# A 64x64 triangular inverse by back substitution on VectorE, corner block included, in a FoX / RWKV-7 layer

## The chip, the cores and the metric

The kernel runs on one core of one Trainium2 chip. A core has a matrix engine (TensorE, PE in the profile, with its weight loads as PEld), VectorE (DVE), ScalarE (ACT), GpSimd (POOL), and SyncE (SP), whose queue issues nearly all transfers. The metric is the device time of one execution in microseconds (us). Before the change the median of three runs is 1895.11 us (1894.64 to 1896.51).

## The reference

One layer over 256 tokens of width 4096. A joint input projection feeds 16 attention heads with a forget gate (FoX, head width 128), 32 RWKV-7 heads (head width 64) and a gate; the gated outputs go through an output projection, a residual and a LayerNorm.

```
proj = x @ w_in                       # 4096 -> fox q|k|v|f, rwkv r|k|v|w_down|a_down, gate z
fox  = softmax(q k^T / sqrt(128) + c_t - c_s, causal) v        # c = cumsum(log_sigmoid(f + f_bias))
S_t  = S_{t-1} diag(w_t) + (S_{t-1} a_t) b_t^T + v_t k_t^T      # 64x64 state of each rwkv head
y_t  = S_t r_t                        # then GroupNorm per head, plus a bonus term
out  = concat(fox, rwkv) * silu(z) @ w_out
x    = LayerNorm(ALPHA * x + out)
```

The recurrence of the RWKV heads is computed in chunks of 64 tokens. In a chunk the terms S a of the 64 tokens depend on each other through a strictly triangular 64x64 matrix N; the kernel forms (1 - N)^-1 for each head and chunk, called X, and then needs only matrix products.

## The kernel before

**Staging.** The 4096-deep projections are products of 128x128 by 128x512 on PE. Every operand is split in two parts, a rounded one (h) made by ScalarE and the rest (l) made by VectorE, and each product is done as three (h h, l h, h l). The weights stream in as tiles of 128x1024 (two steps of the depth): loaded by SP into `raw` buffers (tag `wr`, 6 of them, in `load` and `fetch`), split by `split` into `wh` (4 buffers) and `wl` (3). A tile feeds twelve products.

The input projection runs as 8 groups of 4 blocks (`block(n, b)`), 512 columns each. Group n carries the columns of two FoX heads and of four RWKV heads, as two pairs u = 0, 1 of heads j = 0, 1. `unload` turns a block's result and stores it to memory and back, to have the tokens along the free axis. Then the output projection goes over 8 column blocks of 16 tiles (`project`).

**Side work.** Between the products of the projections stands the work on the heads: `prepare(i)` forms decays and scaled keys of one pair (with `front`), `rwkv(n)` does the chunked recurrence of the four heads of a group ("pass n", 8 passes), `fox(i)` one attention head, `gate` multiplies by the gate, splits and stores a 128-column piece `hl` (29 of the 32 pieces go to memory and come back as `h`; the last three stay).

**The pass.** `rwkv(n)` forms gp, the products of keys with keys and queries of a chunk, masks them into gb and lt, and sends the diagonal 32x32 blocks of N through memory (`nd`) to a layout (`nb`, tag `Nb`) in which 16 matrices lie over the 128 partitions, 8 partitions each, four columns per partition. There the back substitution runs: 31 steps of a multiply (`prod <- Nb, xc`) and a reduction (`xc <- prod`) on VectorE, for two head pairs at once, on 8 columns of each: four of the inverse of a diagonal block, and four of the product of that inverse with the corner block of N, which comes through `zd`. The two results go back through memory (`td`, `qd`) into the tile `TQ`. VectorE transposes the T part into the diagonal blocks of X; TensorE multiplies Q by the other diagonal block (`xp`: 16 products of 32x32 per pass, two instructions each), and ScalarE and VectorE copy that into the corner of X. Then the chunks follow in order: a residual R (`rh`), u = X R (`up`), the state (`sp`), and for all four chunks together the output `yp`. In the first chunk the residual is done in four halved products per pass, beside the xp products; in the later chunks by two full ones per pass.

`residual`, for c > 0 and for c = 0:

```
for u in range(2):
    nc.tensor.matmul(rh[:, u * P : (u + 1) * P], both[:, u, c, 0].rearrange("p j t -> p (j t)"), states[:, :, u, c, :], start=True, stop=True)
...
for u in range(2):
    for j in (1, 0):
        nc.tensor.matmul(rh[HALF[j], u * C : (u + 1) * C], lt[j][:, u, c, 0], SV[j][:, u, c, :], start=True, stop=True)
```

**What sets the order.** Nothing is issued while the program above runs. The class `Later` records every operation of every engine with a duration that it works out from its shape, and `flush` then plans a start for each: at every moment the engine that is free first takes the ready operation with the smallest key. The key is the place of recording, with the splits of weights put far ahead. The generators (`prepare`, `rwkv`, `fox`, `unload`) yield at each `slot()`, two of which stand in each tile, so how often one yields sets its keys. `ROWS` is how many steps of the substitution are recorded in one slot. Side products on PE that follow each other are planned as one run; a change of tile shape on PE costs in the plan. All operations are issued in the planned order by one line of `flush`, line 372, which is why every row of the profile names L372.

Buffers are tiles with a tag; two tiles of a tag share its buffers. `lt`, `BK`, `eL`, `sums` and `above` have one buffer each, `t` five.

**The end.** The output projection needs all pieces h, and the last ones come from pass 7. So `outs` lists first the tiles 0 to 13 (`CUT`) of column blocks 0 and 1, then the first `EARLY` tiles of block 2, and only then tiles 14 and 15 of blocks 0 and 1. When block 0 is complete, the memory of the side work is closed and that of the LayerNorm opened; `load_tok(b)` loads what the residual and LayerNorm of block b need.

Of the kernel before, what the change touches and what calls it, by code (L numbers as in the profile page):

```python
# [19 lines left out]
P = 128  # L20
# [22 lines left out]
EARLY = 4  # L43
BACK = 10
ROWS = 1
# [423 lines left out]
def layer(ctx: ExitStack, tc: tile.TileContext, xt, xtok, w_first, w_main, muv, w_o, up, par, mulora, fbias, lng, lnb, cst, out):  # L469
# [109 lines left out]
    sums = const.tile([P, B], F32, name="sums")  # L579
    nc.gpsimd.memset(sums, 0.0)  # L580
    above = const.tile([P, B // 2], F32, name="above")
    nc.gpsimd.memset(above, 0.0)
# [86 lines left out]
    def rt(name):  # L669
        return t256("t", name, 5)  # L670
# [32 lines left out]
    def lora():  # L703
# [5 lines left out]
        u = rp.tile([NF, S], F32, tag="t", name="fu", bufs=5)  # L709
# [15 lines left out]
    def forget():  # L725
        def ft(name):
            return rp.tile([NF, S], F32, tag="t", name=name, bufs=5)
# [10 lines left out]
        rest = rp.tile([B, S], F32, tag="t", name="frest", bufs=5)  # L738
# [13 lines left out]
        turned_sums = rp.tile([B, S], F32, tag="t", name="fturned", bufs=5)  # L752
# [19 lines left out]
    def gate(y, key, k):  # L772
# [5 lines left out]
        pool, tag, bufs = (rp, "hl", 4) if far else (xpool, f"x{k}", 1)  # L778
# [20 lines left out]
    def add_up(squares):  # L799
# [7 lines left out]
    def spread(name):  # L807
# [26 lines left out]
    def front(i):  # L834
# [21 lines left out]
        eL = rp.tile([P, NCH, C + 1], F32, tag="eL", name=f"eL{i}")  # L856
# [13 lines left out]
    def prepare(i):  # L870
# [21 lines left out]
        add_up(flat(sb))  # L892
# [3 lines left out]
        d = spread(f"sq{i}")  # L896
# [22 lines left out]
    def rwkv(n):  # L919
# [27 lines left out]
        nd = dram.tile([2, 4, NCH, B, B], F32, tag="nd", name=f"nd{n}", bufs=2)  # L947
        nb = rp.tile([P, 2, B, B], F32, tag="Nb", name=f"Nb{n}")
# [28 lines left out]
        prod = rp.tile([P, 2, 2 * NJ, B], F32, tag="prod", name=f"prod{n}")  # L977
        nc.gpsimd.memset(prod[:, :, NJ:], 0.0)
        for j in range(2):
            nc.sync.dma_start(out=prod[C * j : C * j + B, :, NJ:].rearrange("p u k s -> p u (k s)"), in_=zd[j].rearrange("u c (g k) s -> (c g) u (k s)", g=NG))  # L980
# [23 lines left out]
        xc = rp.tile([P, 2, 2 * NJ, B], F32, tag="xc", name=f"xc{n}")  # L1004
        ev = cs[:, C_E : C_E + P].rearrange("p (j s) -> p j s", s=B)
        for u in range(2):
            nc.scalar.copy(prod[:, u, :NJ], ev)
            nc.scalar.copy(xc[:, u, :, B - 1 : B], prod[:, u, :, B - 1 : B])
        for t, s in enumerate(range(B - 2, -1, -1)):
            w = B - 1 - s  # L1010
            nc.vector.tensor_tensor(prod[:, :, :, s + 1 :], nb[:, :, s : s + 1, s + 1 :].to_broadcast([P, 2, 2 * NJ, w]), xc[:, :, :, s + 1 :], ALU.mult)
            nc.vector.tensor_reduce(xc[:, :, :, s : s + 1], prod[:, :, :, s:], AX.X, ALU.add)
# [3 lines left out]
        td, qd = (dram.tile([4, 2, NCH, B, B], F32, tag=t, name=f"{t}{n}", bufs=2) for t in ("td", "qd"))  # L1016
        TQ = rp.tile([P, 2, 2 * NCH, B], F32, tag="prod", name=f"TQ{n}")
        T, Q = (TQ[:, z].rearrange("p (u c) s -> p u c s", u=2) for z in range(2))
# [22 lines left out]
        for a in range(4):  # L1041
            o = C * (a // 2) + B * (a % 2)
            rows = slice(B * a, B * (a + 1))
            nc.vector.transpose(X[rows].rearrange("p u c t -> p (u c) t")[:, :, o : o + B], T[rows].rearrange("p u c s -> p (u c) s"))
        def residual(c):
            rh = pst(f"rh{n}_{c}")
            R = rp.tile([P, 2, C], F32, tag="R", name=f"R{n}_{c}", bufs=2)
            if c:
                for u in range(2):
# [524 lines left out]
```

## Time and profile before

| | us |
|---|---|
| median of three runs | 1895.11 |
| the profiled execution, whole | 1894.52 |
| its span, first to last instruction | 1892.7 |
| PE busy | 1885.3 |
| DVE busy | 1452.0 |
| ACT busy | 975.0 |

The profile is of one execution. A row of its groups reads: line, engine, operation, output <- inputs by name (buffer numbers left out), shapes, count | busy us, mean ns of one | idle time of the engine just before them, and what ended it. A row of a timeline reads: start and length in us from the span's start, engine, line, operation, output <- inputs, shape, count, and in brackets the idle time before it. Rows of PE overlap, since products are pipelined: what a run of products costs is read from the starts of its neighbours. `acc` and `oacc` are the accumulators of the input and the output projection; w_5h and wo_5h are the h parts of weight tile 5.

### The profile page before, as it was taken

To read this page: it belongs to the slowest core of one execution; us is meant where nothing else is said; L and a number is where in the kernel's file an instruction comes from. 1 tells how busy PE (TensorE), PEld (TensorE's weight loads), DVE (VectorE), ACT (ScalarE), POOL (GpSimd) and SP (SyncE) were. 2 spreads that over 40 slices of the span, in tenths; PEclk is the share of its full clock that TensorE was granted. 3 is DMA by queue.
4 is the path that set the end of the run, shared out by engine and by line. 5 is a ranking of instruction groups with operands and counts; after the bars stand their busy time and mean duration, and the time that the engine had idled before them with its cause. 6 is when DMAs were issued, how large, how long until landed. Compare 5 with 4: busy or idle time off the path is not lost.

```text
span 1892.7 us, 27577 instructions
## 1 busy us (share of the span) xinstructions
PE 1885.3 (100%) x9562; PEld 1577.5 (83%) x9562; DVE 1452.0 (77%) x2421; ACT 975.0 (52%) x1496; POOL 41.3 (2%) x98
## 2 busy tenths in 40 slices
PE   9999999999999999999999999999999999999998
PEld 9988888888888888888888888888888888888887
DVE  6598868886887689769876897698768976765556
ACT  6464456446544654455445544654465445443342
POOL 0000000000000000000000000000000000000000
PEclk9999999999999999999999999999999999999999
DMA  9779877977798679867987798679867996966663
GB/s 348 215 218 261 238 202 226 281 224 211 232 268 240 196 238 265 242 190 236 265 241 197 231 274 233 195 238 267 239 197 227 342 295 207 311 214 197 190 199 145
DMA packets 360913, 446.49 MB, mean 236 GB/s; under 512 B 222002, under 2 KB 261652, under 8 KB 360772
## 3 DMA queue, kind: packets, MB, share of 16 engines
q1 hardware_dynamic: 360484, 444.35, 77.7%
q8 instruction: 75, 1.23, 0.3%
q14 instruction: 66, 0.54, 0.1%
q10 hardware_dynamic: 288, 0.37, 0.1%
HBM read 404.69 MB, written 39.93 MB: 235 GB/s over the span
## 4 chain that ended last, share of the span: by engine, by line
PE 99%; DVE 0%; DMA 0%; DVEq 0%; issue 0%; SPq 0%; ACT 0%
PE acc L372 73%; PE oacc L372 18%; PE accl L372 2%; PE gp L372 1%; PE yp L372 1%; PE rh L372 1%; PE up L372 1%; PE lp L372 1%; PE sp L372 1%; PE fop L372 1%; PE fsp L372 0%; PE side L372 0%; PE xp L372 0%; DMA fr<-in_w_first_dram 0%; DVE res L372 0%; PE wp L372 0%
## 5 line engine op out<-in xcount | busy, mean ns | idle before, releaser
L372 DVE TENSOR_TENSOR prod<-Nb,xc 128x16 f32<-128x16 f32 (+30 forms) x248 | 104.8, 423 | 13.6 <-ACT xc L372 7.9
L372 DVE TENSOR_REDUCE xc<-prod 128x16 f32<-128x32 f32 (+30 forms) x248 | 107.5, 434 | 4.5
L372 PE MATMUL acc<-w_5h,x 128*128 128x512 f32 x248 | 77.9, 393 | 0.0
L372 PE MATMUL acc<-w_11h,x 128*128 128x512 f32 x248 | 77.7, 392 | 0.0
L372 PE MATMUL acc<-w_0h,x 128*128 128x512 f32 x248 | 77.7, 392 | 0.0
L372 PE MATMUL acc<-w_10h,x 128*128 128x512 f32 x248 | 77.6, 391 | 0.0
L372 PE MATMUL acc<-w_2h,x 128*128 128x512 f32 x248 | 77.6, 391 | 0.0
L372 PE MATMUL acc<-w_6h,x 128*128 128x512 f32 x248 | 77.5, 392 | 0.0
L372 PE MATMUL acc<-w_9h,x 128*128 128x512 f32 x248 | 77.2, 391 | 0.0
L372 PE MATMUL acc<-w_14h,x 128*128 128x512 f32 x248 | 77.1, 392 | 0.0
L372 PE MATMUL acc<-w_1h,x 128*128 128x512 f32 x248 | 77.0, 390 | 0.0
L372 PE MATMUL acc<-w_12h,x 128*128 128x512 f32 x248 | 77.0, 392 | 0.0
L372 PE MATMUL acc<-w_15h,x 128*128 128x512 f32 x248 | 77.0, 391 | 0.0
L372 PE MATMUL acc<-w_8h,x 128*128 128x512 f32 x248 | 76.8, 391 | 0.0
L372 PE MATMUL acc<-w_4h,x 128*128 128x512 f32 x248 | 76.8, 391 | 0.0
L372 PE MATMUL acc<-w_13h,x 128*128 128x512 f32 x248 | 76.8, 391 | 0.0
L372 PE MATMUL acc<-w_7h,x 128*128 128x512 f32 x248 | 76.7, 390 | 0.0
L372 PE MATMUL acc<-w_3h,x 128*128 128x512 f32 x248 | 76.7, 390 | 0.0
L372 ACT CAST w_11h<-w 128x1024 fp32r<-128x1024 f32 x31 | 32.7, 1054 | 46.7 <-PE acc L372 39.2
L372 ACT CAST w_6h<-w 128x1024 fp32r<-128x1024 f32 x31 | 32.6, 1053 | 46.8 <-PE acc L372 43.7
L372 ACT CAST w_7h<-w 128x1024 fp32r<-128x1024 f32 x31 | 32.7, 1054 | 43.3 <-PE acc L372 39.9
L372 PEld LDWEIGHTS acc<-w_0h,x 128*128 128x128 f32 x248 | 46.6, 188 | 10.0 <-DVE vx L372 0.4
(651 smaller groups left out, 5435.2 us busy)
## 6 DMA issues: line engine op xcount, KB each, us to landing
w<-in_w_main_dram SPq DMA_DIRECT2D x496, 512.0 KB
wo<-in_w_o_dram SPq DMA_DIRECT2D x128, 512.0 KB
bt<-bk SPq DMA_DIRECT2D x96, 128.0 KB
fr<-in_w_first_dram SPq DMA_DIRECT2D x14, 720.0 KB
Nb<-nd SPq DMA_DIRECT2D x16, 512.0 KB
hd<-hl SPq DMA_DIRECT2D x29, 256.0 KB
h<-hd SPq DMA_DIRECT2D x29, 256.0 KB
raw<-bt SPq DMA_DIRECT2D x16, 256.0 KB
```

What stands on the lines that cost most here:

```text
L372: ins = op.call(*op.args, **op.kwargs)
```

## The change

The substitution runs over the whole 64x64 triangular matrix. `nb` now holds three 32x32 blocks of each matrix (upper diagonal, corner, lower diagonal), for 16 matrices at once. A first loop of 31 steps solves the two diagonal blocks on four columns each (half as many columns as before); a second loop of 32 steps goes on upward through the corner block, over 32 to 63 elements of four columns. The result has all three blocks of X: TensorE's product xp, its two copies, the tiles Q and qd, the corner's way through zd and its transposes fall away. X is written by six transposes instead of four. The residual of the first chunk is formed as in the later chunks, by full products with the states, whose own half is zero there.

Around it: `ROWS` goes from 1 to 2 and `EARLY` from 4 to 12; `sums` and `above` become three sets (one for each pair in `prepare`, one for the end of a pass); `t` gets seven buffers and `eL` two; `wr` goes down to five and `hl` to three; the tiles of LayerNorm statistics move to the memory opened at the end; load_tok(2) is called at step 26 of block 2 instead of step 12.

```diff
-EARLY = 4
+EARLY = 12
-ROWS = 1
+ROWS = 2
...
-    sums = const.tile([P, B], F32, name="sums")
...
+    totals = []
+    for n in range(3):
+        totals.append((const.tile([P, B], F32, name=f"sums{n}"), const.tile([P, B // 2], F32, name=f"above{n}")))
...
-            raw = wpool.tile([P, 1024], F32, tag="wr", name=name, bufs=6)
+            raw = wpool.tile([P, 1024], F32, tag="wr", name=name, bufs=5)
...
-        return t256("t", name, 5)
+        return t256("t", name, 7)
...
-        pool, tag, bufs = (rp, "hl", 4) if far else (xpool, f"x{k}", 1)
+        pool, tag, bufs = (rp, "hl", 3) if far else (xpool, f"x{k}", 1)
...
-        eL = rp.tile([P, NCH, C + 1], F32, tag="eL", name=f"eL{i}")
+        eL = rp.tile([P, NCH, C + 1], F32, tag="eL", name=f"eL{i}", bufs=2)
...
-            for a in range(4):
-                o = B * (a % 2)
-                nc.sync.dma_start(out=nd[u, a].rearrange("c r s -> r c s"), in_=gb[a // 2][B * a : B * (a + 1), u, :, o : o + B])
-            if u:
-                gt = rp.tile([P, 2 * NCH, B], F32, tag="xc", name=f"gt{n}")
-                zd = dram.tile([2, 2, NCH, B, B], F32, tag="zd", name=f"zd{n}", bufs=2)
-                for j in range(2):
-                    a = slice(C * j, C * j + B)
-                    nc.vector.transpose(gt[a], gb[j][a].rearrange("p u c t -> p (u c) t")[:, :, B:C])
-                    nc.sync.dma_start(out=zd[j].rearrange("u c k s -> k (u c) s"), in_=gt[a])
-            nc.sync.dma_start(out=flat(nb[:, u]), in_=nd[u].rearrange("q c r s -> (q c) (r s)").unsqueeze(1).to_broadcast([16, NG, B * B]))
+        for j in range(2):
+            upper, lower = slice(C * j, C * j + B), slice(C * j + B, C * j + C)
+            nc.sync.dma_start(out=nd[:, :, j, :, :2].rearrange("u c r b s -> r (u c) (b s)"), in_=gb[j][upper].rearrange("p u c t -> p (u c) t")[:, :, :C])
+            nc.sync.dma_start(out=nd[:, :, j, :, 2].rearrange("u c r s -> r (u c) s"), in_=gb[j][lower].rearrange("p u c t -> p (u c) t")[:, :, B:C])
+        nc.sync.dma_start(out=nb.rearrange("p r b s -> p (r b s)"), in_=nd.rearrange("u c j r b s -> (u c j) (r b s)").unsqueeze(1).to_broadcast([16, NG, 3 * B * B]))
...
         for t, s in enumerate(range(B - 2, -1, -1)):
             w = B - 1 - s
-            nc.vector.tensor_tensor(prod[:, :, :, s + 1 :], nb[:, :, s : s + 1, s + 1 :].to_broadcast([P, 2, 2 * NJ, w]), xc[:, :, :, s + 1 :], ALU.mult)
-            nc.vector.tensor_reduce(xc[:, :, :, s : s + 1], prod[:, :, :, s:], AX.X, ALU.add)
+            nc.vector.tensor_tensor(prod[:, :, :, s + 1 :], nb[:, s, 0:3:2, s + 1 :].unsqueeze(2).to_broadcast([P, 2, NJ, w]), ends[:, :, :, s + 1 :], ALU.mult)
+            nc.vector.tensor_reduce(ends[:, :, :, s : s + 1], prod[:, :, :, s:], AX.X, ALU.add)
+            yield from step(t)
+        wide = rp.tile([P, NJ, 2 * B], F32, tag="prod", name=f"wide{n}")
+        rows2, cols2 = nb.rearrange("p r b s -> p r (b s)"), xc.rearrange("p j b s -> p j (b s)")
+        for t, s in enumerate(range(B - 1, -1, -1)):
+            w = 2 * B - 1 - s
+            nc.vector.tensor_tensor(wide[:, :, :w], rows2[:, s, s + 1 : 2 * B].unsqueeze(1).to_broadcast([P, NJ, w]), cols2[:, :, B + s + 1 :], ALU.mult)
+            nc.vector.tensor_reduce(cols2[:, :, B + s : B + s + 1], wide[:, :, :w], AX.X, ALU.add)
+            yield from step(t)
...
-        for d, cols in ((td, slice(0, NJ)), (qd, slice(NJ, 2 * NJ))):
-            for u in range(2):
-                nc.sync.dma_start(out=d[:, u].rearrange("q c (g j) s -> q (c g) (j s)", g=NG), in_=flat(xc[:, u, cols]))
-        for a in range(4):
-            nc.sync.dma_start(out=TQ[B * a : B * (a + 1), 0], in_=td[a].rearrange("u c r s -> r (u c) s"))
+        nc.sync.dma_start(out=td.rearrange("u c j (g k) b s -> (u c j g) (k b s)", g=NG), in_=xc.rearrange("p j b s -> p (j b s)"))
         for j in range(2):
-            nc.sync.dma_start(out=TQ[C * j + B : C * j + C, 1], in_=qd[2 * j].rearrange("u c k s -> k (u c) s"))
+            nc.sync.dma_start(out=T[C * j : C * j + B].rearrange("p g b s -> p g (b s)"), in_=td[:, :, j, :, :2].rearrange("u c k b s -> k (u c) (b s)"))
+            nc.sync.dma_start(out=T[C * j + B : C * j + C, :, 1], in_=td[:, :, j, :, 2].rearrange("u c k s -> k (u c) s"))
...
-            for u in range(2):
-                for j in (1, 0):
-                    nc.tensor.matmul(rh[HALF[j], u * C : (u + 1) * C], lt[j][:, u, c, 0], SV[j][:, u, c, :], start=True, stop=True)
-            nc.vector.tensor_copy(flat(R), rh[:, : 2 * C])
...
-        xp = pst(f"xp{n}")
-        for u in range(2):
-            for c in range(NCH):
-                for j in range(2):
-                    a, b = slice(C * j, C * j + B), slice(C * j + B, C * j + C)
-                    nc.tensor.matmul(xp[a, u * P + c * B : u * P + (c + 1) * B], Q[b, u, c, :], X[b, u, c, C * j + B : C * j + C], start=True, stop=True)
...
-            if b > 1 and k == 4 + 2 * EARLY * (b == 2):
+            if b > 1 and k == (2 * EARLY + 2 if b == 2 else 4):
```

More of the change, by code (lines that the diff above doesn't have):

```diff
@@ L578, in layer @@
     nc.vector.memset(gneps, GN_EPS)
-    sums = const.tile([P, B], F32, name="sums")
-    nc.gpsimd.memset(sums, 0.0)
-    above = const.tile([P, B // 2], F32, name="above")
-    nc.gpsimd.memset(above, 0.0)
+    totals = []
+    for n in range(3):
+        totals.append((const.tile([P, B], F32, name=f"sums{n}"), const.tile([P, B // 2], F32, name=f"above{n}")))
+        for t in totals[n]:
+            nc.gpsimd.memset(t, 0.0)
     sides = []
@@ L708, in lora @@
         issue(lt2, d[:6].rearrange("(j b) i m a t -> (b i) j (m a t)", j=2))
-        u = rp.tile([NF, S], F32, tag="t", name="fu", bufs=5)
+        u = rp.tile([NF, S], F32, tag="t", name="fu", bufs=7)
         issue(u, d[6, :NF].rearrange("i m a t -> i (m a t)"))
@@ L726, in ft @@
         def ft(name):
-            return rp.tile([NF, S], F32, tag="t", name=name, bufs=5)
+            return rp.tile([NF, S], F32, tag="t", name=name, bufs=7)
         u = ff[0]
@@ L737, in forget @@
         nc.scalar.activation(lg, e1, AF.Ln)
-        rest = rp.tile([B, S], F32, tag="t", name="frest", bufs=5)
+        rest = rp.tile([B, S], F32, tag="t", name="frest", bufs=7)
         nc.vector.memset(rest, 0.0)
@@ L751, in forget @@
         nc.sync.dma_start(out=ncd, in_=lg)
-        turned_sums = rp.tile([B, S], F32, tag="t", name="fturned", bufs=5)
+        turned_sums = rp.tile([B, S], F32, tag="t", name="fturned", bufs=7)
         nc.vector.transpose(turned_sums, whole)
@@ L797, in flat, with add_up @@
         return t.rearrange("p a b -> p (a b)")
-    def add_up(squares):
+    def add_up(squares, sums, above):
         n = B // 2
@@ L805, in add_up, with spread @@
         nc.vector.tensor_tensor(sums[:, :n], sums[:, :n], above, ALU.add)
-    def spread(name):
+    def spread(name, sums):
         nc.vector.transpose(sums, sums)
@@ L891, in prepare @@
         yield
-        add_up(flat(sb))
+        sums, above = totals[u]
+        add_up(flat(sb), sums, above)
         yield
@@ L895, in prepare @@
         nc.vector.reciprocal(sums[:, :NG], sums[:, :NG])
-        d = spread(f"sq{i}")
+        d = spread(f"sq{i}", sums)
         BK = q["BK"][:, u]
@@ L946, in rwkv @@
         gv = [[gp[u][j].rearrange("p (c t) -> p c t", t=P) for j in range(2)] for u in range(2)]
-        nd = dram.tile([2, 4, NCH, B, B], F32, tag="nd", name=f"nd{n}", bufs=2)
-        nb = rp.tile([P, 2, B, B], F32, tag="Nb", name=f"Nb{n}")
+        nd = dram.tile([2, NCH, 2, B, 3, B], F32, tag="nd", name=f"nd{n}", bufs=2)
+        nb = rp.tile([P, B, 3, B], F32, tag="Nb", name=f"Nb{n}")
         for u in range(2):
@@ L1003, in rwkv, with step @@
         other = turns()
-        xc = rp.tile([P, 2, 2 * NJ, B], F32, tag="xc", name=f"xc{n}")
+        prod = rp.tile([P, 2, NJ, B], F32, tag="prod", name=f"prod{n}")
+        xc = rp.tile([P, NJ, 3, B], F32, tag="xc", name=f"xc{n}")
         ev = cs[:, C_E : C_E + P].rearrange("p (j s) -> p j s", s=B)
-        for u in range(2):
[L1007 to L1010, printed above, removed]
-            nc.vector.tensor_tensor(prod[:, :, :, s + 1 :], nb[:, :, s : s + 1, s + 1 :].to_broadcast([P, 2, 2 * NJ, w]), xc[:, :, :, s + 1 :], ALU.mult)
-            nc.vector.tensor_reduce(xc[:, :, :, s : s + 1], prod[:, :, :, s:], AX.X, ALU.add)
+        ends = xc.rearrange("p j b s -> p b j s")[:, 0:3:2]
+        for h in range(2):
+            nc.scalar.copy(prod[:, h], ev)
+            nc.scalar.copy(ends[:, h, :, B - 1 : B], ev[:, :, B - 1 : B])
+        def step(t):
             next(other, None)
@@ L1041, in rwkv @@
         for a in range(4):
-            o = C * (a // 2) + B * (a % 2)
             rows = slice(B * a, B * (a + 1))
-            nc.vector.transpose(X[rows].rearrange("p u c t -> p (u c) t")[:, :, o : o + B], T[rows].rearrange("p u c s -> p (u c) s"))
+            for b in range(a % 2, 2):
+                o = C * (a // 2) + B * b
+                nc.vector.transpose(X[rows].rearrange("p u c t -> p (u c) t")[:, :, o : o + B], T[rows, :, b])
         def residual(c):
@@ L1047, in residual @@
             R = rp.tile([P, 2, C], F32, tag="R", name=f"R{n}_{c}", bufs=2)
[L1048 to L1053 removed]
             for u in range(2):
[L1055 to L1070 removed]
+                nc.tensor.matmul(rh[:, u * P : (u + 1) * P], both[:, u, c, 0].rearrange("p j t -> p (j t)"), states[:, :, u, c, :], start=True, stop=True)
+            for j in (1, 0):
+                nc.vector.tensor_copy(R[HALF[j]], rh[HALF[j], : 2 * P].rearrange("p (u j v) -> p u j v", u=2, j=2)[:, :, j, :])
+            return R
         R = residual(0)
@@ L1114, in rwkv @@
             nc.scalar.mul(yc[:, u], yp[:, u * S : (u + 1) * S], column("gn_gain", i0 + u))
-        add_up(flat(sd))
+        sums, above = totals[2]
+        add_up(flat(sd), sums, above)
         nc.scalar.activation(sums[:, : B // 2], sums[:, : B // 2], AF.Sqrt, scale=1.0 / HD, bias=gneps)
         nc.vector.reciprocal(sums[:, : B // 2], sums[:, : B // 2])
-        d = spread(f"var{n}")
+        d = spread(f"var{n}", sums)
         yield from wait(W["vs"])
@@ L1286, in layer @@
     late = []
-    st = [const.tile([P, NB + m, 6], F32, name=f"lst{m}") for m in range(2)]
+    st = []
     split_k = KT - 2 * LATE + WHOLE - 1
@@ L1393, in layer @@
             lminus = rpool.tile([P, OB], F32, name="lminus")
+            st.extend(rpool.tile([P, NB + m, 6], F32, name=f"lst{m}") for m in range(2))
             lneps = const.tile([P, 1], F32, name="lneps")
```

21 lines of the change are left out of this document (4 added, 17 removed).

## The prediction

> **What bounds the kernel now.** I read the first page first: who is busy, and what the chain that ended last is made of.
>
> ```profile
> span 1892.7 us, 27577 instructions
> ...
> PE 1885.3 (100%) x9562; PEld 1577.5 (83%) x9562; DVE 1452.0 (77%) x2421; ACT 975.0 (52%) x1496; POOL 41.3 (2%) x98
> ...
> PE 99%; DVE 0%; DMA 0%; DVEq 0%; issue 0%; SPq 0%; ACT 0%
> ```
>
> PE fills the span and 99% of the chain of waits. The list of PE's waits says that it is starved nowhere in the middle:
>
> ```profile
> PE warmup L372 <- POOL idle L372: 1.0, 1, 1.0
> PE accl L372 <- ACT wf1h L372: 0.4, 1, 0.4
> ```
>
> So time falls only by what PE has less to do, and rises only where PE is made to wait for the first time. DVE is next: over a stretch in which a back substitution runs it is nearly full, and it splits the weights that PE needs.
>
> ```profile
> 1100.00:1150.00 50.00, 50.00 (x225) 41.47 (x224) 47.75 (x93) 23.59 (x34) 0.00 (x0) 1.00 0.86 253
> ```
>
> (Columns: stretch, length, then busy time and count of PE, PE's weight loads, DVE, ACT, POOL.) The change takes work from PE and gives more to DVE, so the question is whether DVE stays off PE's path.
>
> **PE, removed.** The timeline of PE around pass 1's last product shows the divided run: 16 small products in 32 instructions, and the four halved products of the first residual in eight:
>
> ```profile
> 425.96 0.39 PE L372 MATMUL acc<-w_12l,x 128*128 128x512 f32 x1
> 426.27 0.69 PE L372 MATMUL xp<-X,TQ 32*32 32x32 f32 x32
> 426.90 0.45 PE L372 MATMUL rh<-SV,lt 128*64 128x64 f32 x8
> 427.28 0.73 PE L372 MATMUL acc<-w_12h,x 128*128 128x512 f32 x2
> 427.85 0.40 PE L372 MATMUL acc<-w_12l,x 128*128 128x512 f32 x1
> ```
>
> The busy times overlap, so I measure the displacement of the main products, from start to start. Undisturbed, one group of three and one tile of twelve take:
>
> ```profile
> 1589.97 0.61 PE L372 MATMUL oacc<-wo_8h,h 128*128 128x512 f32 x2
> ...
> 1590.65 0.61 PE L372 MATMUL oacc<-wo_8h,h 128*128 128x512 f32 x2
> ...
> 1592.69 0.61 PE L372 MATMUL oacc<-wo_9h,h 128*128 128x512 f32 x2
> ```
>
> A group is 0.68 us, a tile 2.72 us. From 425.96 to 427.85 are 1.89 us, so the divided run costs 1.89 - 0.68 = **1.21 us**, the two changes of shape included.
>
> **PE, added.** The first residual becomes what the later ones are, four full-width instructions. One of those, alone:
>
> ```profile
> 806.22 0.61 PE L372 MATMUL acc<-w_13h,x 128*128 128x512 f32 x2
> 806.67 0.61 PE L372 MATMUL rh<-SV,lt 128*128 128x128 f32 x4
> ...
> 807.35 0.62 PE L372 MATMUL acc<-w_13h,x 128*128 128x512 f32 x2
> ```
>
> 1.13 - 0.68 = **0.45 us**. Net 0.76 us per pass, 8 passes: **-6.1 us**. Bounds: -7 where the residual lands behind another side run and shares its entry, -5 where the plan cuts side work into a few more runs.
>
> The Trainium skill, "TensorE: Matmul & The Clock Gate", Measured speedup vs the span model, says that packed tiles start about 4 ns apart. That would make the 32 instructions 0.19 + 31 x 0.004 = 0.31 us, the removed run some 0.3 us cheaper, and the net some -3.6 us. The rows disagree: these 32 starts spread over 426.27 to 426.90, 20 ns each, and the displacement counts whatever the spacing is, so I keep -6.1.
>
> **DVE.** The old loop runs 31 pairs on 16 columns; the new ones run 31 pairs on 8 columns and 32 pairs on 4 columns of 32 to 63 elements.
>
> ```profile
> L372 DVE TENSOR_TENSOR prod<-Nb,xc 128x16 f32<-128x16 f32 (+30 forms) x248 | 104.8, 423 | 13.6 <-ACT xc L372 7.9
> L372 DVE TENSOR_REDUCE xc<-prod 128x16 f32<-128x32 f32 (+30 forms) x248 | 107.5, 434 | 4.5
> ```
> ```profile
> 536.43 0.19 DVE L372 TENSOR_TENSOR prod<-Nb,xc 128x16 f32<-128x16 f32 x1 [2.07 <-ACT xc L372]
> ...
> 587.44 0.67 DVE L372 TENSOR_TENSOR prod<-Nb,xc 128x496 f32<-128x496 f32 x1
> ```
>
> The two groups give (104.8 + 107.5) / 8 = 26.5 us per pass. The two sizes give 0.48 us for 480 elements: 1.0 ns per element and 0.17 us fixed; 62 instructions over 16368 elements then make 26.9, as measured. New: 8 x (496 + 527) = 8184 elements and 4 x 2 x 1520 = 12160, 126 instructions: 126 x 0.17 + 20.3 = **41.7 us, +15.2 per pass**. The other DVE edits cancel: two transposes of the corner block, one copy of the product and one whole residual copy go, two more transposes into X and two half copies come.
>
> ```profile
> L372 DVE STREAM_TRANSPOSE X<-TQ 32x256 f32<-32x256 f32 x32 | 13.9, 435 | 0.8
> L372 DVE COPY R<-rh 64x128 f32<-64x128 f32 x48 | 13.9, 289 | 1.6 <-PE rh L372 0.5
> L372 DVE COPY X<-xp 32x256 f32<-32x256 f32 x8 | 3.4, 422 | 8.5 <-ACT X L372 5.5 <-PE xp L372 3.0
> ```
>
> In all some 121 us more, DVE 1452 to 1573 of 1889, 83%. There is room on average, none inside a substitution. There the steps take turns with weight splits, so it stretches. The last pass:
>
> ```profile
> 1479.41 0.19 DVE L372 TENSOR_TENSOR prod<-Nb,xc 128x16 f32<-128x16 f32 x1 [0.62 <-ACT xc L372]
> ...
> 1529.35 0.64 DVE L372 TENSOR_REDUCE xc<-prod 128x16 f32<-128x512 f32 x1
> ...
> 1544.03 1.83 DVE L372 STREAM_TRANSPOSE X<-TQ 32x256 f32<-32x256 f32 x4
> ```
>
> 50.6 us for 26.5 us of steps. Lower bound of the stretch +15 (the added time alone), upper 41.7 x 50.6 / 26.5 = 80, +29; I take +29, as splits come through the whole run. Behind it the chain is shorter: from 1530.0 to the first use of X at 1550.2 are 20 us, with ten transfers in it, now five, and without the product and its two copies. Bounds -3 (product and copies alone, 1547.5 to 1550.2) and -8; I take -6. A pass thus ends some **23 us later** after its start (12 to 26).
>
> **What hides that.** Two covers. First, the loop from pass to pass. Two more groups of blocks lie at
>
> ```profile
> 663.36 41.73 PE acc L372 x184
> ...
> 1039.78 41.73 PE acc L372 x184
> ```
>
> (chain of waits, two groups apart), so a group is 188.2 us. Pass 2's last product and pass 3's first are 63 us apart:
>
> ```profile
> 641.58 0.29 PE L372 MATMUL yp<-gb,UV 128*64 128x64 f32 x4
> ...
> 705.02 2.06 PE L372 MATMUL gp<-lt,BK 64*128 64x128 f32 x32
> ```
> ```profile
> 657.18 0.98 DVE L372 SCALAR_TENSOR_TENSOR s<-raw,prm,s 128x255 f32<-128x255 f32 x2
> ...
> 702.88 0.99 DVE L372 SCALAR_TENSOR_TENSOR BK<-s,prm,ae 64x256 f32<-64x256 f32 x2
> ```
>
> Of those 63 us what truly follows the last product is the writing of lt, two products per head pair, a copy and gp, below 10 us; the preparation between 657 and 704 waits for the projected block (raw) and for few buffers (one eL, five t, one sums), of which the change makes more. So 23 us fit into 63 and the slip doesn't add up from pass to pass. Second, the end. The last hl is made at 1611.0 and read at 1619.15:
>
> ```profile
> 1611.03 0.42 DVE L372 TENSOR_TENSOR hl<-h,hl 128x256 fp32r<-128x256 f32 x1
> ...
> 1619.15 0.62 PE L372 MATMUL oacc<-wo_14h,hl 128*128 128x512 f32 x2
> ```
>
> 7.7 us to spare, and EARLY 12 puts eight more tiles, 8 x 2.72 = 21.8 us, ahead of it: 29.5 us of cover for a slip of 23. Without the tiles PE would wait some 15 us. The output block's own work is only moved; load_tok(2)'s five transfers, one ACT and two DVE instructions now come three tiles (8 us) before the block ends, moved on SP past seven of the block's own weight loads; its user (the add of block 2) frees banks that PE wants a whole block later.
>
> **Raw weight buffers, 6 to 5.** SP may issue a load one tile (2.72 us) later. In the last group, where the h tiles come back, casts do wait for weights:
>
> ```profile
> 1516.52 1.05 ACT L372 CAST wo_1h<-wo 128x1024 fp32r<-128x1024 f32 x1 [2.60 <-DMA wo<-in_w_o_dram]
> ```
> ```profile
> 1523.59 0.62 PE L372 MATMUL oacc<-wo_1h,h 128*128 128x512 f32 x2
> ```
>
> The cast ends 6.0 us before PE reads it, so 2.7 us less costs nothing; if that cover were gone too, at most about 3 us, once.
>
> **SP and the rest.** Per pass 24 issues become 10 (nd 8 to 4, zd 2 and its return 2 gone, Nb 2 to 1, stores 4 to 1, loads 6 to 4); Nb is half a MB larger. SP and DMA gain a little; nothing of it is on PE's path: 0. The third sums set, hl 4 to 3 and the moved statistics tiles add no instruction to PE: 0, hidden under PE's matmuls.
>
> **Sum.** The profiled execution took 1894.52 us (span 1892.7 and 1.8 around it); 1894.5 - 6.1 = 1888.4. It lies 0.6 us under the median 1895.11, so the median should be **1889.0**.
>
> **Rivals.** A measurement here tells 0.2%, 3.8 us, from nothing.
>
> (a) *Slower: the loop of passes closes.* If the preparation still cannot start before the old pass ends (its 47 us between 657 and 704 stay behind it), a lap takes 705.0 - 641.6 = 63 plus the pass, 124 us now (1457.85 to 1581.9 in the last one) plus 23: 210 against 188. It decides from a lap above 188.2. For it: those 47 us are filled with work on DVE and ACT that the plan has placed there. Against: 16 of the 63 us, from 641.6 to 657.2, are a wait for raw, which PE's blocks time. At 3 us over the period a lap, seven laps add 21 to 23, less 29.5 of cover: PE waits 14 us before the last tiles, 1903. Chance 0.14.
>
> (b) *No change: the gain is given back.* DVE at 47.75 of 50 delays splits when the plan's durations are a little short, and the thinner raw queue adds to it; a pause of 0.5 us in each pass and 2 at the h transfers takes back 6: 1895 (1892 to 1897). Against: today PE never waits even there, and splits run two to three tiles ahead. Chance 0.15.
>
> (c) *The chain grows only by the added time and side runs merge better*: -7 at most, since PE has no other idle time to give: 1888. It is inside the forecast.
>
> **Chances.** Forecast 0.71, (a) 0.14, (b) 0.15. Its own range is 1887 to 1891; to leave out no more than 2 in 10 I go from 1886 to 1899, which takes (b) and the start of (a). Faster 0.71, same 0.13, slower 0.16 (all of (a) and the end of (b)).
>
> **What would show it.** Right: no xp rows; rh 128 instructions, all of full shape; PE's busy time some 6 us less and still no waits in the middle; DVE near 1573; the two loops some 42 us per pass and spread over 65 to 80; the last hl some 10 to 35 us later than 1611 and still ahead of its reader. Wrong: a PE wait on hl before tiles 14 and 15 (a); PE waits on split weights inside substitutions (b); gp of successive passes more than 188.2 us apart.

## The result and the profile after

The changed kernel takes 1920.62 us (median; 1916.40 to 1922.71), the kernel before beside it 1895.61: a ratio of 1.0132 [1.0117, 1.0147], 25 us slower, where 6 us faster was forecast. The page of the changed kernel (span, busy times, the chain's shares):

```profile
span 1920.8 us, 27292 instructions
...
PE 1896.2 (99%) x9274; PEld 1580.4 (82%) x9274; DVE 1544.5 (80%) x2933; ACT 968.2 (50%) x1488; POOL 44.4 (2%) x94
...
PE 79%; DMA 10%; DVE 8%; issue 2%; ACT 1%; SPq 0%; DVEq 0%; ACTq 0%; POOL 0%; POOLq 0%
```

TensorE's share of the chain of waits falls from 99% to 79%; transfers now make 10% of it and VectorE 8%. The list of PE's waits gives for each the total, the times and the longest. Before it held 1.6 us in three entries, one at the very end and the others in the first 8 us; now it begins so (`w_15h` and `w_10l` are parts of weight tiles, `bk` is the copy that empties a finished accumulator, `fsp` the scores of an attention head with its operands `qx` and `kx`):

```profile
PE acc L372 <- ACT bk L372: 4.4, 5, 1.6
PE gp L372 <- DVE BK L372: 3.1, 4, 1.8
PE acc L372 <- ACT w_15h L372: 1.8, 1, 1.8
PE acc L372 <- DVE w_10l L372: 1.8, 5, 0.4
PE fsp L372 <- DVE kx L372: 1.4, 2, 1.2
PE fsp L372 <- DVE qx L372: 1.2, 1, 1.2
```

By their times in the trace they fall into three kinds. The waits at gp and on `w_10l` come before Nb's transfer is issued. Those on `bk`, and on the split tiles `w_15` and `w_0`, come 16 to 20 us behind its issue, when the fourth block of a group starts and the substitution is in its first steps. Those at `fsp` come later, in the middle of a substitution or near its end. The worst place is in pass 1; here are the timelines of SyncE, ScalarE and TensorE, one piece of the chain of waits (start, length, what), and windows of 5 us:

```profile
328.54 1.61 SPq L372 DMA_DIRECT2D Nb<-nd  x1
330.20 0.58 SPq L372 DMA_DIRECT2D w<-in_w_main_dram  x1
...
333.97 11.31 SPq L372 DMA_DIRECT2D w<-in_w_main_dram  x1
...
346.47 1.04 ACT L372 CAST w_15h<-w 128x1024 fp32r<-128x1024 f32 x1 [10.72 <-DMA w<-in_w_main_dram]
...
347.57 0.73 PE L372 MATMUL acc<-w_15h,x 128*128 128x512 f32 x2 [1.85 <-ACT w_15h L372]
348.83 0.79 PE L372 MATMUL acc<-w_15l,x 128*128 128x512 f32 x1 [0.53 <-DVE w_15l L372]
```
```profile
330.20 16.17 DMA w<-in_w_main_dram
```
```profile
345.00:350.00 5.00, 2.63 (x9) 1.54 (x8) 4.04 (x16) 2.61 (x3) 0.00 (x0) 0.82 0.81 173
350.00:355.00 5.00, 5.00 (x14) 3.84 (x13) 4.76 (x13) 3.06 (x4) 0.00 (x0) 0.50 0.98 302
355.00:360.00 5.00, 5.00 (x23) 4.12 (x22) 4.83 (x13) 2.11 (x2) 0.00 (x0) 1.00 1.11 324
```

Nb's transfer is issued at 328.5. The load of weight tile 15 is issued right behind it, at 330.20, and by the chain it lands 16.17 us later; its cast waits 10.72 us for it, and TensorE for the cast. (The issue at 333.97, which takes 11.31 us on SyncE, is that of a load two tiles further on; the cast of that tile doesn't wait for it.) In the 5 us after the stall the granted clock is 0.50 and 14 products pass in place of 23, so the pause is paid a second time.

Counting, between neighbouring main products, what goes beyond their undisturbed spacing of 0.2267 us (a twelfth of a tile) gives the whole account from the two traces (us):

```
                                   before   after
gaps over 0.3 us, no side product     0      14.2
main products, all smaller excess   14.1     23.2   (mostly the clock)
side products and their waits       99.0    103.0   (6.1 less of work was forecast)
```

14 + 9 + 4 = 27 of the 28 us between the two spans: small stalls, the clock behind them (13.7 us at 0.50, which is 6.8 us of work), and waits at side products that more than use up the work saved.

The volume that the prediction set at nothing, in the transfer list (before, then after), and the stretch of pass 4 (windows of before, of after):

```profile
Nb<-nd SPq DMA_DIRECT2D x16, 512.0 KB
```
```profile
Nb<-nd SPq DMA_DIRECT2D x8, 1536.0 KB
```
```profile
900.00:950.00 50.00, 50.00 (x225) 41.48 (x224) 44.01 (x85) 23.44 (x34) 0.00 (x0) 1.00 0.90 263
```
```profile
900.00:950.00 50.00, 48.08 (x210) 38.73 (x209) 43.65 (x92) 22.13 (x26) 0.00 (x0) 1.00 0.99 277
```

1.0 MB per pass became 1.5. The DMA share (the column before the last) was 0.90 in that stretch and is 0.99; over the span it is 79%, which hides it. The share alone doesn't tell a loss, though: in the run below that loses nothing (1.0 MB, no second loop) it is 0.89 in this stretch, and 1.05 in its first half.

### The profile page after: what moved, and what is told of

It reads as the page before. It is cut to its first block, busy times and chain, and to the rows that moved or that the text cites. A ratio compares the mean times of both kernels' runs of the same rounds, so it can differ in the third digit from the quotient of the medians.

```text
span 1920.8 us, 27292 instructions
## 1 busy us (share of the span) xinstructions
PE 1896.2 (99%) x9274; PEld 1580.4 (82%) x9274; DVE 1544.5 (80%) x2933; ACT 968.2 (50%) x1488; POOL 44.4 (2%) x94
## 4 chain that ended last, share of the span: by engine, by line
PE 79%; DMA 10%; DVE 8%; issue 2%; ACT 1%; SPq 0%; DVEq 0%; ACTq 0%; POOL 0%; POOLq 0%
PE acc L372 54%; PE oacc L372 18%; DMA w<-in_w_main_dram 4%; PE accl L372 2%; DMA Nb<-nd 1%; DMA sq<-sums 1%; DMA vs<-vd 1%; PE yp L372 1%; PE rh L372 1%; DMA vv<-vt 1%; DVE prod L372 1%; DVE xc L372 1%; PE up L372 1%; DVE vs L372 1%; PE lp L372 1%
## 5 line engine op out<-in xcount | busy, mean ns | idle before, releaser
L372 DVE TENSOR_TENSOR wide<-Nb,xc 128x128 f32<-128x128 f32 (+31 forms) x256 | 90.6, 354 | 4.0
L372 DVE TENSOR_REDUCE xc<-wide 128x4 f32<-128x128 f32 (+31 forms) x256 | 88.8, 347 | 4.3
L372 DVE TENSOR_TENSOR prod<-Nb,xc 128x8 f32<-128x8 f32 (+30 forms) x248 | 71.9, 290 | 23.5 <-DMA Nb<-nd 17.6
L372 DVE TENSOR_REDUCE xc<-prod 128x8 f32<-128x16 f32 (+30 forms) x248 | 72.8, 293 | 5.8
L372 ACT CAST w_10h<-w 128x1024 fp32r<-128x1024 f32 x31 | 32.7, 1053 | 55.8 <-PE acc L372 31.7
```

The source lines that it names most:

```text
L372: ins = op.call(*op.args, **op.kwargs)
```

## The experiments

Times are medians with the kernel before run beside them (1894.8 to 1896.0). Theory N: the 0.5 MB more of Nb per pass make the weights late. Rivals: R, the sixth raw buffer; P, a plan that is too tight; D, the second loop on VectorE. The edits are shown in part; "..." marks what is left out.

**The raw buffer alone** (in the kernel before).

```diff
-            raw = wpool.tile([P, 1024], F32, tag="wr", name=name, bufs=6)
+            raw = wpool.tile([P, 1024], F32, tag="wr", name=name, bufs=5)
```

> The kernel before, with five raw weight buffers instead of six and nothing else. Theory R (the changed kernel starves because one raw buffer less takes 2.7 us from the lead of every weight load): 1905 to 1918. Theory D (VectorE's second loop delays the splits and all that stands around them): 1894 to 1898, as before. Theory N (the single Nb transfer of 1.5 MB holds up the weight loads behind it): 1894 to 1898.

Measured 1898.72, ratio 1.0015 [1.0006, 1.0025]: 3 us, not 25.

**The raw buffer given back, room taken from t and s** (in the changed kernel).

```diff
-        return t256("t", name, 7)
+        return t256("t", name, 5)
...
-        r = t256(f"s{n}", f"s{n}_{i}", 2)
+        r = t256(f"s{n}", f"s{n}_{i}", 1)
...
-            raw = wpool.tile([P, 1024], F32, tag="wr", name=name, bufs=5)
+            raw = wpool.tile([P, 1024], F32, tag="wr", name=name, bufs=6)
```

> The changed kernel with the sixth raw buffer back; its room is taken from t (seven to five buffers) and from the lerped r and k (two to one each). Theory R: 1889 to 1898, most of the loss gone. Theory D: 1914 to 1922. Theory N: 1912 to 1920, a little better, since a longer queue of raw tiles rides over a late transfer.

Measured 1970.0, 1.0394 [1.0379, 1.0410]. It says nothing on raw, but something on the other buffers. PE's longest wait:

```profile
PE oacc L372 <- ACT hl L372: 17.4, 1, 17.4
```

That is what the prediction's rival (a), the loop of passes closing, would show: with fewer buffers for the preparation the last piece is late at the end. Since `s` was cut below the kernel before as well, the run doesn't tell whether the added buffers of `t` alone prevent it.

**The second loop left out** (the corner of the inverse stays zero).

```diff
+        nc.gpsimd.memset(xc[:, :, 1], 0.0)
...
-            nc.vector.tensor_tensor(wide[:, :, :w], rows2[:, s, s + 1 : 2 * B].unsqueeze(1).to_broadcast([P, NJ, w]), cols2[:, :, B + s + 1 :], ALU.mult)
-            nc.vector.tensor_reduce(cols2[:, :, B + s : B + s + 1], wide[:, :, :w], AX.X, ALU.add)
```

> The changed kernel without the 64 instructions of the second loop: the corner block of the inverse is left out (filled with zeros on GpSimd), all transfers, buffers and other instructions stay. Theory D: 1887 to 1893, below the kernel before by the products that TensorE no longer does. Theories R and N: 1912 to 1920, as the stalls sit before and at the start of the first loop, which stays.

Measured 1912.81, 1.0086 [1.0069, 1.0103]: only 7.8 us come back, so D alone isn't it. A stall in pass 3, in the timelines of SyncE, ScalarE and TensorE (the loads of tiles 1 and 2 are issued at 723.74 and 726.57, between the rows shown):

```profile
721.14 0.35 SPq L372 DMA_DIRECT2D w<-in_w_main_dram  x1
...
723.15 0.54 SPq L372 DMA_DIRECT2D Nb<-nd  x1
...
730.28 5.20 SPq L372 DMA_DIRECT2D w<-in_w_main_dram  x1
...
735.68 1.05 ACT L372 CAST w_1h<-w 128x1024 fp32r<-128x1024 f32 x1 [5.51 <-DMA w<-in_w_main_dram]
737.59 1.05 ACT L372 CAST w_2h<-w 128x1024 fp32r<-128x1024 f32 x1 [0.86 <-DMA w<-in_w_main_dram]
738.54 1.07 ACT L372 COPY bk<-acc 128x512 f32<-128x512 f32 x2
...
739.17 0.50 PE L372 MATMUL acc<-w_0h,x 128*128 128x512 f32 x1 [1.35 <-ACT bk L372]
```

ScalarE takes its work in order: the casts wait for weights, the copy that empties the finished accumulator (bk) stands behind them, and TensorE, which has split weights in hand, waits for that bank. The same wait, `acc <- bk`, leads the changed kernel's list.

**Nb in two transfers of 0.75 MB**, rows 16 to 31, which the loops use first, ahead.

```diff
-        nc.sync.dma_start(out=nb.rearrange("p r b s -> p (r b s)"), in_=nd.rearrange("u c j r b s -> (u c j) (r b s)").unsqueeze(1).to_broadcast([16, NG, 3 * B * B]))
+        for part in reversed(range(2)):
+            r = slice(part * (B // 2), (part + 1) * (B // 2))
+            nc.sync.dma_start(out=nb[:, r].rearrange("p r b s -> p (r b s)"), in_=nd[:, :, :, r].rearrange("u c j r b s -> (u c j) (r b s)").unsqueeze(1).to_broadcast([16, NG, 3 * B * B // 2]))
```

> The changed kernel with the Nb transfer cut in two of 0.75 MB by rows, the upper rows (used first) ahead. Theory N: 1900 to 1910. Theories R and D: within 4 us of 1920.

Measured 1915.16, 1.0102 [1.0087, 1.0117]: 5.4 us come back, less than N forecast and a little more than the others; the rest stays.

**Nb without the corner block, and no second loop** (1.0 MB as before; corner zero), with five and with six raw buffers.

```diff
...
-        nb = rp.tile([P, B, 3, B], F32, tag="Nb", name=f"Nb{n}")
+        nb = rp.tile([P, B, 2, B], F32, tag="Nb", name=f"Nb{n}")
...
```

> As the run without the second loop (1912.8), and the corner block isn't loaded either: Nb is 1 MB instead of 1.5 MB per pass, still one transfer; the corner of the inverse is left out. Theory N (the 1.5 MB of Nb hold up the weight loads): 1899 to 1906. Theory R (five raw buffers): 1910 to 1914. Theory P (the plan puts gp and the first steps that need a landing closer to the landing than the queue allows, now that the preparation comes earlier): 1907 to 1912.

> The same with the sixth raw buffer back, which fits into the room of the smaller Nb. Theory R: 1889 to 1897. Theories N and P: 2 to 4 us below the run with five buffers, as five cost the kernel before 2.8 us.

Measured 1892.08, 0.9983 [0.9973, 0.9992], and 1892.15, 0.9982 [0.9973, 0.9991]. Against the 1912.81 above, 0.5 MB per pass are 20.7 us. R falls: with five buffers the loss is gone, and the sixth gives nothing more. Whether a sixth would ride over the late loads at 1.5 MB wasn't shown. Page, waits and pass 3 of the first:

```profile
PE 1881.5 (100%) x9274; PEld 1575.7 (83%) x9274; DVE 1396.0 (74%) x2421; ACT 972.5 (51%) x1490; POOL 45.5 (2%) x102
```
```profile
PE acc L372 <- ACT bk L372: 1.1, 1, 1.1
```
```profile
711.80 0.82 SPq L372 DMA_DIRECT2D Nb<-nd  x1
...
722.55 1.05 ACT L372 CAST w_2h<-w 128x1024 fp32r<-128x1024 f32 x1 [3.04 <-DMA w<-in_w_main_dram]
723.51 1.16 ACT L372 COPY bk<-acc 128x512 f32<-128x512 f32 x2
```

The casts wait for weights here too, 3.04 us at most around this copy in place of 5.51, and that is inside the lead that the splits have.

**More hold in the plan** (P), alone and with Nb in four transfers.

```diff
-MARGIN = 1000
+MARGIN = 2500
...
```

> The changed kernel, and the plan holds what waits for another engine back by 2.5 us instead of 1 us after the planned end (3.75 instead of 1.5 us after a landing); no instruction differs, only the order. Theory P: 1900 to 1910, with fewer waits of PE before gp and fsp. Theories R and N: 1916 to 1922.

> The changed kernel with Nb in four transfers of rows and the longer hold of 2.5 us. Theories N and P together: 1893 to 1903. Theory R: 1912 to 1918.

Measured 1994.12, 1.0515 [1.0499, 1.0530], and 1980.54, 1.0444 [1.0428, 1.0459]. Holding side products back lengthens the passes until the end waits for hl (17 us at once in both, as above). P is no remedy.

**The bytes, read by nobody.** The 1.0 MB kernel without loop, and the kernel before with five raw buffers, each with 0.5 MB more into an unread tile.

```diff
...
+        more = rp.tile([P, B * B], F32, tag="more", name=f"more{n}")
+        nc.sync.dma_start(out=more, in_=nd.rearrange("u c j r b s -> (u c j) (r b s)")[:, B * B :].unsqueeze(1).to_broadcast([16, NG, B * B]))
...
```

> The changed kernel without the second loop and with the two diagonal blocks alone in its Nb transfer (1 MB; the corner of the inverse is left at zero), which took 1892.1 us, and behind that transfer a second one of 0.5 MB into a tile that nobody reads; gp stands at tile 7 of the third block in passes 2 to 7, as without it. With all 1.5 MB in one transfer it was 1912.8 us. If the bytes cost: 1906 to 1914 us. If it is the one long transfer, or the loop's waiting for the end of it: 1894 to 1901 us. In between, by the kernel before with the same third transfer (+6.6 us): 1899 us.

> The kernel before with five raw buffers, and behind its two Nb transfers a third one of the same kind and size (0.5 MB) into a tile that nothing reads; computation, side work and vector loops are those of before. Without the third transfer this kernel took 1898.7 us. Theory N (the volume broadcast per pass, in a stretch where the DMA engines are full anyway, delays weights and so TensorE): the 20.7 us that 0.5 MB less took off the changed kernel come back here for the most part, 1908 to 1922 us, with TensorE waiting on casts that wait on the weights. Rival L (it is not the volume: what lost the time in the changed kernel is the later start of its own loop, which reads all of the 1.5 MB): nobody reads the third transfer, so 1897 to 1902 us.

Measured 1908.14, 1.0066 [1.0051, 1.0081], and 1905.32, 1.0049 [1.0034, 1.0064]. In the changed kernel's plan a transfer that nobody waits for costs 16 us of the 20.7, so most of the price is that of the bytes, and not of a later start of the loop that reads them. In the plan of before they cost 6.6, against a forecast of 9 to 23. There side products wait (2.5 us, first row) and the bank doesn't, while the waits of the other kernel (second row) are those of the changed one:

```profile
PE fsp L372 <- DVE kx L372: 2.5, 3, 1.5
```
```profile
PE acc L372 <- ACT bk L372: 7.6, 4, 3.2
```

Why the old plan bears the same bytes better isn't settled. Its three transfers of 0.5 MB with weight loads between them, and gp at tile 8 of the third block in place of 5 to 7, are the visible differences.

**Nb on a queue of its own** (issued by GpSimd).

```diff
-        nc.sync.dma_start(out=nb.rearrange("p r b s -> p (r b s)"), in_=nd.rearrange("u c j r b s -> (u c j) (r b s)").unsqueeze(1).to_broadcast([16, NG, 3 * B * B]))
+        nc.gpsimd.dma_start(out=nb.rearrange("p r b s -> p (r b s)"), in_=nd.rearrange("u c j r b s -> (u c j) (r b s)").unsqueeze(1).to_broadcast([16, NG, 3 * B * B]))
```

> The changed kernel with the one Nb transfer issued by GpSimd on a queue of its own, in place of SyncE's queue; volume and everything else as in the changed kernel (1920.6 us). Theory N in its form 'the engines are full' (what counts is the bytes moved in that stretch): 1912 to 1926 us, about the same. Rival Q (the weights stand behind the 1.5 MB in one queue, in order, and are late only by that): the weights overtake, TensorE's waits on casts go, 1893 to 1905 us.

Measured 1918.9, 1.0131 [1.0107, 1.0154]: nothing gained. The weights aren't late by standing behind Nb in one queue. What both forms have in common is the bytes on the DMA engines, so the form of N in which those are full is left. The Trainium skill, "DMA: Bandwidth & Descriptors", Issuing engines are not separate DMA queues, says that transfers of different issuing engines run on the same 16 DMA engines and interleave; this run agrees.

**Fewer unread values sent** (rows 16 to 31 as 64 values each, 1.25 MB in two transfers).

```diff
...
-        nb = rp.tile([P, B, 3, B], F32, tag="Nb", name=f"Nb{n}")
...
+        nb = rp.tile([P, B // 2, 3, B], F32, tag="Nb", name=f"Nb{n}")
+        na = rp.tile([P, B // 2, 4, B // 2], F32, tag="Na", name=f"Na{n}")
...
```

> The changed kernel with less of the unread triangles sent: rows 16 to 31 of each matrix as 64 instead of 96 values (0.5 MB, first), rows 0 to 15 as before (0.75 MB, second), so 1.25 MB per pass in two transfers in place of 1.5 MB in one, and four small stores more; the loops read the same values. Theory N, linear in the volume: 0.25 MB less is half of 20.7 us, 1920.6 - 10 = 1910 us, less up to 5 for the earlier start that two transfers gave: 1904 to 1912. If only the start of the loop counts and not the volume: like the split in two, 1914 to 1917 us.

Measured 1914.89, 1.0104 [1.0088, 1.0119], no better than the split in two: in this form 0.25 MB bought nothing. Whether the price of a byte isn't linear here, or the four more stores took the gain back, isn't shown.

**The loop at 1.0 MB**, whole and with every second step (the corner is another than the reference's). The edit of the 1.0 MB kernel above, but with the loop kept; the lines shown are those of the second run alone.

```diff
...
-        for t, s in enumerate(range(B - 1, -1, -1)):
+        for t, s in enumerate(range(B - 1, -1, -2)):
...
```

> The changed kernel with only the two diagonal blocks brought in (1 MB per pass, five raw buffers), but with the second loop of 32 steps kept in full on VectorE; it reads the lower diagonal block where the corner block belongs, so the corner of the inverse comes out other than in the reference. Without that loop this took 1892.1 us. If volume and loop add up (20.7 us for the volume, 7.8 us for the loop in the changed kernel): 1898 to 1902 us. If the loop costs only where transfers are late already (the weights late and VectorE full together): 1891 to 1895 us, below the kernel before. If the loop is the larger cause and the volume only shifted it: 1905 or more.

> The changed kernel with 1 MB in Nb and every second step of the second loop alone (16 pairs, some 11 us of VectorE per pass in place of 22; the corner of the inverse is not that of the reference). No loop was 1892.1, the whole loop 1907.9 us. If VectorE's time costs in proportion: 1898 to 1902 us. If there is room for some of it and the price comes above that (VectorE full only with the whole loop): 1891 to 1895 us. If already the order that any second loop brings into the plan costs: 1905 to 1910 us.

Measured 1907.92, 1.0066 [1.0051, 1.0081], and 1904.14 (1900.08 to 1906.13), 1.0042 [1.0027, 1.0057]. So the loop costs 15.8 us where the volume is small, and half of it some 12 already, more than its share of the time: either no part of the vector time is free, or a part of the price is that of the order that any second loop brings into the plan. These two weren't told apart. One stretch of the kernel without loop and with it, 590 to 600 us:

```profile
590.00:600.00 10.00, 10.00 (x56) 8.60 (x55) 5.05 (x9) 5.41 (x14) 0.72 (x2) 1.00 0.93 249
```
```profile
590.00:600.00 10.00, 10.00 (x48) 8.33 (x48) 9.72 (x22) 4.78 (x7) 0.70 (x1) 1.00 0.94 214
```

Where VectorE used to have half of its time free (5.05 of 10), it is full (9.72). Its slack went, and TensorE's longest waits are on vector work:

```profile
PE gp L372 <- DVE BK L372: 3.5, 6, 0.9
PE fsp L372 <- DVE qx L372: 1.8, 2, 1.1
```

**gp planned later** (theory G: the loop costs only because the plan with it sets gp ahead of its transfer).

```diff
-W = {"fo": 3, "vs": 2, "np": 2, "gp": 5, "tp": 4, "d1": 8, "d2": 12, "xp": 3, "fs": 4, "fp": 5}
+W = {"fo": 3, "vs": 2, "np": 7, "gp": 5, "tp": 4, "d1": 8, "d2": 12, "xp": 3, "fs": 4, "fp": 5}
```

> The changed kernel with 1 MB in Nb and the second loop (on the lower block in place of the corner's values), 1907.9 us, with one number of the plan changed: the use of n<-sq is recorded seven steps behind its issue in place of two, by which gp comes at tile 8 of the third block in place of tile 5, where the kernel before has it. Theory G (the loop costs because gp is planned ahead of its transfer and TensorE waits for BK): TensorE's waits for BK go (3.5 us in the list, about 8 us with what gp displaces), 1895 to 1901 us. Rival D (VectorE's 15 us more per pass cost wherever gp stands): 1904 to 1912 us.

> The changed kernel with the same one number changed (use of n<-sq seven steps behind its issue), all 1.5 MB and the corner as in the changed kernel; gp comes at tiles 7 and 8 in place of 5 and 6. Theory G: TensorE's waits for BK go, the waits on casts and bk at the start of the fourth block stay or grow, since Nb then comes later, nearer to that start: 1908 to 1916 us. Rival D: 1917 to 1925 us.

> The changed kernel with 1.25 MB in two transfers (1914.9 us) and the same one number changed, gp at tile 8. Theory G: the 3.7 us of waits for BK and what comes with them go, 1903 to 1909 us; still above the kernel before, since the weights' waits stay. Rival D: 1912 to 1918 us.

Measured 1909.11, 1.0065 [1.0048, 1.0081]; 1933.73, 1.0196 [1.0181, 1.0211]; 1908.65, 1.0069 [1.0047, 1.0091]. In the first the wait at gp is gone, and these have taken its place:

```profile
PE acc L372 <- ACT bk L372: 4.2, 2, 2.9
PE fsp L372 <- ACT qx L372: 3.1, 1, 3.1
PE fsp L372 <- DVE qx L372: 3.0, 3, 1.5
```

The total stays, so at 1.0 MB G falls: gp was where the lateness showed, not what made it. With all 1.5 MB, Nb is issued some 38 to 41 us into the third block in place of 31 to 33, nearer to the next block's start, 13 us are lost, which neither theory had forecast, and the wait for the bank grows:

```profile
PE acc L372 <- ACT bk L372: 12.5, 4, 4.2
```

With 1.25 MB the medians differ by 6 us in favour of the later gp, which is what G had forecast there, but the four runs spread over 10 us (1904.88 to 1914.66), so the third case stays open. It is the best form of the whole change that was run, and still slower than before.

**The same vector time in the kernel before** (32 pairs on tiles of their own, five raw buffers, ROWS 2).

```diff
...
+        wide = rp.tile([P, NJ, 2 * B], F32, tag="wide", name=f"wide{n}")
+        for t, s in enumerate(range(B - 1, -1, -1)):
...
+            nc.vector.tensor_reduce(tail[:, :, s : s + 1], wide[:, :, :w], AX.X, ALU.add)
...
```

> The kernel before with five raw buffers (1898.7 us) and ROWS 2, and behind its substitution 32 more pairs of the sizes of the second loop on a tile of their own that nothing reads: some 22 us of VectorE per pass more, the rest as before. The plan, with one eL and five t, sets gp at tile 13 of the third block in place of 8. If vector time costs wherever it stands, as in the changed kernel: 1912 to 1920 us. If it cost there only by the plan with more buffers: 1898 to 1903 us. If the loop from pass to pass closes without the added buffers (rival a of the prediction), TensorE waits at the last tiles, for hl: above 1920 us.

Measured 1941.6, 1.0251 [1.0211, 1.0290]. Two of the first three waits of PE's list aren't in the changed kernel's:

```profile
PE oacc L372 <- ACT hl L372: 7.3, 1, 7.3
...
PE rh L372 <- DVE SV L372: 4.8, 6, 0.8
```

That is the sign of rival (a) again, as expected for one eL and five t: successive gp lie 191.4 to 194.0 us apart. So this run doesn't give the price of the vector time by itself.

## Why the prediction was wrong

**Right.** *PE, removed and added*: xp and the halved products are gone (9562 to 9274 instructions). By the starts of the main products around it, the run of xp and the halved products displaced 1.10 us in each of the eight passes before, and a run of one full residual alone displaces 0.36 us after. That is 0.74 us a pass and 5.9 us in all, against 6.1 forecast. The Trainium skill's rule that was weighed there ("TensorE: Matmul & The Clock Gate", Measured speedup vs the span model) gave -3.6, and the trace doesn't bear it out: each of the eight runs displaced as much as the one shown. The time shows less of the saving. Without its two costs the changed kernel (1892.08) lies 6.6 us under the kernel before with five raw buffers (1898.72), but that one loses 3 us of its own; with six in both it is 1892.15 against 1894.83, 2.7 us. The side work stands there in 143 runs in place of 134, as the forecast's smaller bound had it. *DVE*: the groups

```profile
L372 DVE TENSOR_TENSOR wide<-Nb,xc 128x128 f32<-128x128 f32 (+31 forms) x256 | 90.6, 354 | 4.0
L372 DVE TENSOR_REDUCE xc<-wide 128x4 f32<-128x128 f32 (+31 forms) x256 | 88.8, 347 | 4.3
L372 DVE TENSOR_TENSOR prod<-Nb,xc 128x8 f32<-128x8 f32 (+30 forms) x248 | 71.9, 290 | 23.5 <-DMA Nb<-nd 17.6
...
L372 DVE TENSOR_REDUCE xc<-prod 128x8 f32<-128x16 f32 (+30 forms) x248 | 72.8, 293 | 5.8
```

give 324.1 / 8 = 40.5 us per pass, forecast 41.7. VectorE's whole busy time rose by 92.5 us, not 121. *What hides that, the end*: the last hl is made at 1661.4 and read at 1668.3,

```profile
1661.00 0.42 DVE L372 TENSOR_TENSOR hl<-h,hl 128x256 fp32r<-128x256 f32 x1 [0.47 <-ACT hl L372]
```
```profile
L372 PE MATMUL oacc<-wo_14h,hl x30: 389/389/389, 1668.3 to 1895.2; 128*128 128x512 f32 x30
```

so EARLY 12 held, with 6.9 us to spare, in part by luck. A pass, from its gp to its yp, was to become 23 us longer (12 to 26) and became 25 to 44 us longer, with substitutions of 82 to 87 us in place of 65 to 80. Against that gp starts 5 to 11 us earlier in its block from pass 2 on, which the forecast hadn't counted. Counted from the start of the third block of the last group, the last hl still comes 31.5 us later, more than the 29.5 us of cover; its reader was put off by 9 us more than the eight tiles by what the kernel lost. Rival (a) came only where buffers were taken away, side work held back or vector time added without the buffers. *Raw weight buffers*: 3 us in the kernel before (the bound given there), nothing at 1.0 MB.

**The step that failed** is "SP and the rest: ... Nb is half a MB larger. SP and DMA gain a little; nothing of it is on PE's path: 0". It counted issues and left the bytes at nothing without a reason. The DMA share was not looked at, though the row of 1100 to 1150 us at the top of the prediction has it: 0.86. In pass 4's stretch the engines stood at 0.90, and the weights need them. With no loop the bytes cost 20.7 us (16 of them shown by bytes that nobody reads); with the loop 1920.62 - 1907.92 = 12.7 us.

**The second miss** is "What hides that": VectorE's added time was asked only whether it delays the pass, and in rival (b) whether it delays splits, by 6 us. It also takes the slack with which VectorE follows the plan: 15.8 us at 1.0 MB, 7.8 at 1.5 MB. The two don't add up; together they are 1920.62 - 1892.08 = 28.5 us. Without them the change is 3.5 us faster than the 1895.61 before, and 28.5 - 3.5 makes the 25.

**The rivals.** (b) had the right kind, late splits and new waits, and its sign came: TensorE waits for split weights in the first steps of two substitutions (347.6 and 1498.2 us). Of its two causes the thinner raw queue gave nothing at 1.0 MB and the full VectorE was one of the two; it didn't name the bytes, and its size was 6 us. The sign named for gp, more than 188.2 us apart, tells little: in the kernel before, successive gp already lie up to 192 us apart. From pass 2 to pass 7 the mean is 189.0 us before and 190.9 us after, which is the time lost and not the closing of a loop.

**Open.** How the loop's price divides between vector time and the order that the plan makes of it (the runs with half the loop range over 6 us, and the kernel before with the added vector time has a cost of its own); why the plan of before bears the unread bytes at two fifths of the price (6.6 us against 16); and why Nb and the loads behind it take 16 us to land at the worst place.

## What to carry to other kernels

Look at the DMA share of the stretch in which a transfer moves, not at the mean, and don't set its bytes to nothing: where the share was 0.9 and TensorE's weights needed the engines, half a MB cost 0.8 to 2.6 us a pass, depending on the plan. A full TensorE with a fixed order lives on the slack of the engines behind it, so work moved to an engine with under a quarter of its time free wasn't free here, and removing one wait from such a plan moved it to the next late result. Before a rearrangement that sends more data, run it without the data and with the data unread: two runs that tell the price of the bytes.

## What was not expected of the hardware

Short stalls can cost twice. Ahead of its last microseconds the granted clock of the changed kernel falls to 0.50 three times: at 348.2 us for 6.8 us, at 515.4 and at 1501.9 us for 3.4 us each. The first fall comes 0.6 us behind the end of a single wait of 1.85 us, and ahead of the second of 0.53 us; the second behind a wait of 1.84 us; the third when several waits had left TensorE idle for 1.8 of the last 3.4 us. The Trainium skill, "TensorE: Matmul & The Clock Gate", What's actually happening, puts the fall to half rate after an idle window of about 3.4 us; the half rate agrees, while here waits of about half that were enough. They don't always bring it: with the bytes that nobody reads (1.0 MB, no second loop), waits of 2.99 and 3.19 us passed with the clock at 1.00.

The issue of a single weight load on SyncE, 0.35 us just ahead of a 1.5 MB transfer, took 5.20 and 11.31 us behind one. In both places the weights that TensorE was then short of had been issued before that, so this isn't what made them late.
